# SSD stage: the sample's in-chunk products join the run of chunks 2 and 3, over two PSUM banks

## The chip, the cores and the metric

The kernel runs on one core of one Trainium2 chip. The metric is device time in microseconds (us) of one execution. Below, PE is TensorE, DVE is VectorE, ACT is ScalarE, POOL is GpSimd, and SP is SyncE, whose queue issues most of the DMAs. PEld in the profile is the weight load that belongs to each matmul.

## The reference, cut to what matters

One decoder layer computes `proj = rmsnorm(x) @ w_in` for 512 prompt tokens and for a sample batch of 8 rows of 8 tokens (64 tokens), runs three branches, merges them and projects. The change is in branch B, the Mamba-2 SSD. It has 32 heads in 8 groups of 4, head dimension 64 and state size 128. Per group and per chunk of 128 tokens:

```
a_cs   = cumsum(dt * a)
y_diag = einsum('bclgn,bcsgn->bgcls', c, b) * exp(a_cs[l] - a_cs[s], l >= s) @ (x * dt)
states = einsum('bcsgn,bgrcs,bcsgrp->cbgrpn', b, exp(a_cs[-1] - a_cs), x * dt)
y_off  = c @ h_prev * exp(a_cs);  h = h * exp(a_cs[-1]) + states
y      = y_diag + y_off + x * d_skip
```

The prompt is chunks 0 to 3. The 64 sample tokens are handled as a fifth chunk, number 4, whose mask keeps the 8 rows apart and whose carried state comes from `state_ssm`.

## The kernel before

The stage before the change's stage normalises x and holds its transpose in two parts (`hn_hi`, `hn_lo`); every large product takes three matmul passes (hi by hi, hi by lo, lo by hi). The SSD stage then goes through the 8 groups. PE's order is written out by hand: a list `units` alternates half jobs of the large products (24 matmuls of 128x288 into an `acc` bank, function `gemm_half`, line 167; some 3.2 us) with lists of SSD steps, the function `steps(g)` (line 778) with twelve of them, `w[0]` to `w[11]`, for each group. The half jobs that run beside group g make the convolution inputs of group g+1 (`conv_job`), the gate z of group g (`z_job`) and, from group 2 on, parts of the output projection (`proj_job`). Weights for a job are loaded two jobs ahead by SP (line 130) and split one job ahead into `whi` (ACT, line 98) and `wlo` (DVE, line 99). The order on DVE, ACT and SP is not written out: a scheduler places their instructions from its own estimate, so it may move work far from the edit. Each engine then runs its list strictly in order.

The steps named in this document, with the lines of the kernel before:

- `decays(g, c)`, lines 480 to 492: a DMA brings the decay exponents of chunk c into a tile `e` (three buffers), DVE adds the mask (L489), ACT takes four exponentials (L491).
- `chunk_cb(g, c)`, line 524: PE forms C by B (L532), DVE multiplies `e` by it (L533). The last instruction is kept as `made`.
- `y_diag(g, cs)`, line 536: for each chunk and each of the four heads one matmul with 64 output partitions (L548, `yps<-e,xdt`). In the trace each of these f32 matmuls shows as two. `run(first, ...)` makes the first matmul wait for the `made` of the other chunks, so that PE does not stop inside the run.
- `y_add`, line 554: DVE adds the bank to `ysb` (L559).
- `c_h0(g, j)`, line 664: eight matmuls with 32 output partitions (L674) into a `yps` bank; ACT copies it out (L678).
- `h0_T`, `h0_new`: transposes of the sample's states (L644), their update (PE L653, ACT L658, DVE L659).
- `gate_y(g-1)`, `norm_y(g-1)`: gate and group norm of the group before; ACT takes Ln (L701) and Exp (L702), with a load of the function table wherever one follows another kind.

There are 8 PSUM banks: 3 `acc`, 2 `yps`, 3 `sps`. In a group `yps` is taken five times, in the order chunks 0 and 1, chunks 2 and 3, `c_h0` 0, `c_h0` 1, chunk 4.

Of the kernel before, what the change touches and what calls it, by code (L numbers as in the profile page):

```python
# [17 lines left out]
P = 128  # L18
# [3 lines left out]
TS = 64  # L22
# [20 lines left out]
def tile_hybrid_step(  # L43
# [8 lines left out]
    V, S, PE, GP, SY = nc.vector, nc.scalar, nc.tensor, nc.gpsimd, nc.sync  # L52
# [21 lines left out]
    def y_tile():  # L74
        return bank["yps"].tile([P, 512], F32, tag="yps", name="yps")
# [42 lines left out]
    def run(first, *made):  # L118

        for m in made:  # L120
            tc.add_manual_dep(first.ins, m.ins.name, mybir.DependencyInfo(
                mybir.DependencyClass.NoSync if m.ins.engine == first.ins.engine else mybir.DependencyClass.Sync,
                mybir.DependencyReason.DATA), reason="run")
# [76 lines left out]
    with ExitStack() as stb:  # L200
# [17 lines left out]
        for i in range(5):  # L218
# [6 lines left out]
            r = rsqrt_(pb, ss[:n], 1.0 / D, EPS, "BT", root=True)  # L225
# [120 lines left out]
        for f in range(2):  # L346
            PE.matmul(rps[:96, 128 + f * H:128 + (f + 1) * H], lhsT=sel[:, f].rearrange("p r t -> p (r t)"),
                      rhs=wdec[:, 4], start=True, stop=True)
# [131 lines left out]
        def decays(g, c):  # L480

            d = st_[g]
            h0_ = 4 * g
            smp = c == 4
            w = TS if smp else P
            e = d["ex", c] = pb.tile([P, 4, P], F32, tag="e", name="e", bufs=3)
            ew = e[:, :, 0:w]
            SY.dma_start(out=ew, in_=a_scr[h0_:h0_ + 4, c * P:c * P + w][None].to_broadcast([P, 4, w]))
            V.tensor_tensor(ew, ew, (tri4 if smp else tri)[:, None, 0:w].to_broadcast([P, 4, w]), ALU.add)  # L489
            for h in range(4):  # L490
                S.activation(e[:, h, 0:w], e[:, h, 0:w], AF.Exp, bias=nacs[:, c, h0_ + h:h0_ + h + 1])  # L491
# [41 lines left out]
            made = V.tensor_tensor(ew, ew, cb[:, None, 0:w].to_broadcast([P, 4, w]), ALU.mult)  # L533
            d["e", c] = e, d.pop(("xdt", c)), made

        def y_diag(g, cs):

            d = st_[g]
            yps = y_tile()
            w = TS if cs[0] == 4 else P  # L540
            y4 = yps[:, 0:2 * len(cs) * w].rearrange("p (c j l) -> p c j l", c=len(cs), j=2)
            parts = [d.pop(("e", c)) for c in cs]
            first = None
            for i, (e, xdt, made) in enumerate(parts):
                for j in range(2):
                    for r in range(2):
                        h = 2 * j + r
                        m = PE.matmul(y4[64 * r:64 * r + 64, i, j], lhsT=xdt[:, h], rhs=e[:, h, 0:w], start=True, stop=True)  # L548
                        first = first or m
            if len(parts) > 1:  # L550
                run(first, *[p[2] for p in parts[1:]])
            return y4

        def y_add(g, cs, y4):
            ysb = st_[g]["ysb"]
            w = y4.shape[3]
            c0 = cs[0] * P
            dst = ysb[:, :, c0:c0 + len(cs) * w].rearrange("p j (c l) -> p c j l", c=len(cs))
            V.tensor_tensor(dst, dst, y4, ALU.add)  # L559
# [25 lines left out]
        def y_off(g, c):  # L585

            d = st_[g]
            c0 = c * P
            hT, ysb = d["hT", c - 1], d["ysb"]
            yo = s_tile()  # L590
            for j in range(2):
                PE.matmul(yo[:, j * P:(j + 1) * P], lhsT=hT[:, 2 * j:2 * j + 2].rearrange("p h d -> p (h d)"),  # L592
                          rhs=d["C"][:, c0:c0 + P], start=True, stop=True)
            t1 = pb.tile([P, 2, P], F32, tag="t1", name="t1", bufs=2)
            V.tensor_tensor(t1, yo[:, 0:256].rearrange("p (j l) -> p j l", j=2), d["ebc"][:, :, c0:c0 + P], ALU.mult)
            ys = ysb[:, :, c0:c0 + P]
            V.tensor_tensor(ys, ys, t1, ALU.add)
# [165 lines left out]
        with tc.manual_schedule(engines={mybir.EngineType.PE}):  # L763
            def group_jobs(g):

                c = [conv_job(g + 1, ci) for ci in range(4)] if g + 1 < G else [gate_job(0), gate_job(1), gate_job(2), gate_job(3)]
                z = [z_job(g, 0), z_job(g, 1)]
                if g < 2:
                    return c + z
                p = [proj_job(g // 2 - 1, 2 * (g % 2) + i) for i in range(2)]  # L770
                if g % 2 == 0:
                    return c + [z[0], p[0], z[1], p[1]]
                return [c[0], p[0], c[1], p[1], c[2], c[3]] + z

            def yd(g, *cs):
                y_add(g, cs, y_diag(g, cs))

            def steps(g):

                w = [[] for _ in range(12)]  # L780
                w[0] = [lambda: start_y(g), lambda: decays(g, 2), lambda: chunk_a(g, 1)]
                w[1] = [lambda: state(g, 0)]
                if g > 0:
                    w[1] += [lambda: y_smp(g - 1), lambda: gate_y(g - 1)]
                w[2] = [lambda: state(g, 1), lambda: chunk_a(g, 2)]
                w[3] = [lambda: y_off(g, 1), lambda: yd(g, 0, 1), lambda: decays(g, 3)]
                w[4] = [lambda: state(g, 2), lambda: chunk_a(g, 3), lambda: decays(g, 4)]
                if g > 0:
                    w[5] = [lambda: norm_y(g - 1)]
                w[5] += [lambda: y_off(g, 2), lambda: chunk_a(g, 4), lambda: h0_load(g, 0)]  # L790
                w[6] = [lambda: state(g, 3), lambda: chunk_t4(g), lambda: h0_load(g, 1)]
                w[7] = [lambda: y_off(g, 3), lambda: chunk_cb(g, 4)]
                w[8] = [lambda: yd(g, 2, 3), lambda: state_out(g), lambda: h0_T(g, 0, 0)]
                w[9] = [lambda: h0_T(g, 0, 1), lambda: h0_new(g, 0, 0), lambda: h0_new(g, 0, 1)]
                w[10] = [lambda: c_h0(g, 0), lambda: h0_T(g, 1, 0), lambda: h0_T(g, 1, 1)]
                if g + 1 < G:
                    w[10] += [lambda: decays(g + 1, 0), lambda: decays(g + 1, 1)]
                w[11] = [lambda: h0_new(g, 1, 0), lambda: h0_new(g, 1, 1)]
                if g + 1 < G:
                    w[11] += [lambda: conv_out(g + 1)]  # L800
                w[11] += [lambda: c_h0(g, 1), lambda: yd(g, 4)]
                return w


            units = [(j, h) for j in (conv_job(0, ci) for ci in range(4)) for h in range(2)]
            units.append((None, [lambda: decays(0, 0), lambda: decays(0, 1)]))
            for g in range(G):
                us = [(j, h) for j in group_jobs(g) for h in range(2)]
                w = steps(g)
                at = range(12) if g < 2 else (0, 1, 3, 4, 6, 7, 9, 10, 11, 13, 14, 15) if g % 2 else (0, 1, 2, 3, 4, 5, 7, 9, 10, 12, 13, 15)  # L810
                at = list(at)
                if g == 0:
                    at = [min(a + 1, 11) for a in at]
                    between = {0: [lambda: chunk_a(0, 0), lambda: conv_out(0)]}
                else:
                    between = {}
                    units.append((None, [lambda g=g: chunk_a(g, 0)]))
                for i, a in enumerate(at):
                    between.setdefault(a, []).extend(w[i])
                for u, x in enumerate(us):  # L820
                    units += [x, (None, between.get(u, []))]
            tail = {0: [lambda: y_smp(G - 1), lambda: gate_y(G - 1)], 5: [lambda: norm_y(G - 1)]}
            for i, u in enumerate([(j, h) for j in (gate_job(jj) for jj in range(4, 8)) for h in range(2)]):
                units += [u, (None, tail.get(i, []))]
            units += [(j, h) for j in (proj_job(3, p) for p in range(4)) for h in range(2)]

            jobs = [u[0] for u in units if u[0] is not None and u[1] == 0]
            at = {id(j): i for i, j in enumerate(jobs)}
            jobs[0].load()
            jobs[0].prep()  # L830
            jobs[1].load()
            for j, h in units:
                if j is None:
                    for w_ in h:
                        w_()
                    continue
                i = at[id(j)]
                if h == 0:
                    if i + 2 < len(jobs):
                        jobs[i + 2].load()  # L840
                    if i + 1 < len(jobs):
                        jobs[i + 1].prep()
                j.half(h)
# [509 lines left out]
    for a in range(2):  # L1353
        r, c = slice(64 * a, 64 * a + 64), slice(512 * a, 512 * a + 512)
# [139 lines left out]
```

## Time and profile before

| what | value |
|---|---|
| median of 3 runs | 1150.23 us (1148.32 to 1156.42) |
| the profiled execution, its own time | 1151.22 us |
| its span, first to last instruction | 1149.5 us |
| mean granted TensorE clock | 0.993 of 2.4 GHz |
| PE busy | 1099.6 us, 96% of the span |
| DVE busy | 781.9 us, 68% |
| ACT busy | 622.1 us, 54% |

The span is shorter than the time by 1.7 us that lie around the instructions. A row of the timeline gives start, duration, engine, line, operation, output and inputs, count, and in brackets the idle time before it with what ended that idle time. "issue" there means that nothing in the profile was waited for.

### The profile page before, as it was taken

The numbers are of one execution on the slowest core, as the hardware profiler recorded it, in microseconds if no ns is written. First come the engines' busy times: TensorE is split into PE (matmuls) and PEld (weight loads), VectorE is DVE, ScalarE is ACT, GpSimd is POOL, SyncE is SP. The second block draws the span as 40 slices with busy tenths as digits, with TensorE's granted clock in tenths as the row PEclk, the third lists the DMA queues.
The fourth block names the chain that finished last, engine by engine and source line by source line (L and its number), as shares of the span: only waits on it lengthen the run. The fifth ranks groups of instructions, "written<-read, shape, count | busy, mean of one in ns | idle before, by whom it ended". The sixth has DMA issues, their size and how long they took to land.

```text
span 1149.5 us, 20445 instructions
## 1 busy us (share of the span) xinstructions
PE 1099.6 (96%) x8199; PEld 1024.1 (89%) x8199; DVE 781.9 (68%) x1450; ACT 622.1 (54%) x1294; POOL 37.7 (3%) x110
## 2 busy tenths in 40 slices
PE   5989999899999989989999999999999999999997
PEld 4989899799998989989999877899999999889776
DVE  5778787748787667866644644786875567775743
ACT  6456686766868456665553244344653236564421
POOL 3010010000000000000000000000000000000000
PEclk9999999999999999999999999999999999999999
DMA  6433544155352524425232525631262353465411
GB/s 190 128 82 111 156 116 138 59 159 145 98 156 84 155 88 126 126 70 169 88 115 95 190 74 165 193 111 52 96 222 101 130 180 102 121 183 197 152 47 73
DMA packets 160462, 144.90 MB, mean 126 GB/s; under 512 B 10160, under 2 KB 141264, under 8 KB 160368
## 3 DMA queue, kind: packets, MB, share of 16 engines
q1 hardware_dynamic: 137264, 126.12, 35.9%
q10 hardware_dynamic: 23104, 17.49, 4.8%
q8 instruction: 64, 1.05, 0.4%
q14 instruction: 30, 0.25, 0.1%
HBM read 124.13 MB, written 19.46 MB: 125 GB/s over the span
## 4 chain that ended last, share of the span: by engine, by line
PE 84%; DVE 6%; ACT 5%; DMA 3%; issue 1%; ACTq 0%; SPq 0%
PE acc L167 32%; PE acc L908 15%; PE acc L154 12%; PE acc L1038 4%; PE acc L1443 4%; PE acc L1103 2%; PE yps L548 2%; DVE cacc L418 1%; PE sps L644 1%; DVE wlo L99 1%; PE sps L503 1%; PE sps L567 1%; PE sps L592 1%; PE yps L674 1%; PE yps L1391 1%
## 5 line engine op out<-in xcount | busy, mean ns | idle before, releaser
L167 PE MATMUL acc<-hn_hi,whi 128*128 128x288 f32 x896 | 272.6, 304 | 1.0 <-ACT thm L732 0.8
L167 PE MATMUL acc<-hn_hi,wlo 128*128 128x288 f32 x896 | 266.2, 297 | 4.1 <-DVE wlo L99 4.1
L167 PE MATMUL acc<-hn_lo,whi 128*128 128x288 f32 x896 | 265.7, 297 | 0.0
L167 PEld LDWEIGHTS acc<-hn_hi,wlo 128*128 128x128 f32 x896 | 169.7, 189 | 4.4 <-DVE wlo L99 4.3
L167 PEld LDWEIGHTS acc<-hn_hi,whi 128*128 128x128 f32 x896 | 170.1, 190 | 3.6 <-ACT thm L732 1.0
L167 PEld LDWEIGHTS acc<-hn_lo,whi 128*128 128x128 f32 x896 | 170.0, 190 | 0.5
L98 ACT CAST w<-wraw 128x1024 fp32r<-128x1024 f32 (+1 forms) x64 | 59.2, 942 | 103.4 <-PE acc L908 24.0
L99 DVE TENSOR_TENSOR wlo<-wraw,whi 128x1024 fp32r<-128x1024 f32 x72 | 87.9, 1221 | 31.8 <-ACT whi L98 31.3
L167 PE MATMUL acc<-hb,whi 128*128 128x288 f32 x512 | 105.2, 301 | 3.1 <-DVE zs L463 2.6
L98 ACT CAST whi<-wraw 128x1024 fp32r<-128x1024 f32 x72 | 75.5, 1049 | 56.1 <-PE acc L167 48.3
L99 DVE TENSOR_TENSOR w<-wraw,w 128x1024 fp32r<-128x1024 f32 x64 | 68.5, 1087 | 36.0 <-ACT w L98 35.9
L908 PE MATMUL acc<-hn_hi,w 128*128 128x288 f32 x512 | 89.5, 300 | 0.0
L908 PE MATMUL acc<-tT,w 128*128 128x288 f32 x576 | 86.1, 298 | 0.0
L167 PEld LDWEIGHTS acc<-hb,whi 128*128 128x128 f32 x512 | 82.7, 191 | 3.7 <-DVE zs L463 2.8
L418 DVE SCALAR_TENSOR_TENSOR cacc<-raw,cwh,cacc 128x600 f32<-128x600 f32 x96 | 80.3, 838 | 4.2 <-ACT cacc L416 3.7
L908 PEld LDWEIGHTS acc<-tT,w 128*128 128x128 f32 x576 | 78.5, 188 | 0.9 <-issue 0.9
L167 PE MATMUL acc<-hb,wlo 128*128 128x288 f32 x256 | 76.0, 297 | 2.8 <-DVE wlo L99 2.8
L908 PEld LDWEIGHTS acc<-hn_hi,w 128*128 128x128 f32 x512 | 74.1, 188 | 2.1 <-DVE thx L926 0.5
L491 ACT ACTIVATE e<-e,nacs 128x128 f32<-128x128 f32 (+1 forms) x160 | 50.3, 386 | 16.4 <-DVE e L489 16.4
L99 DVE TENSOR_TENSOR w<-S,w 128x1024 fp32r<-128x1024 f32 x32 | 39.2, 1224 | 25.1 <-ACT w L98 25.1
L167 PEld LDWEIGHTS acc<-hb,wlo 128*128 128x128 f32 x256 | 48.8, 191 | 3.1 <-DVE wlo L99 3.1
L154 PE MATMUL acc<-ha,w 128*128 128x288 f32 x384 | 51.5, 295 | 0.0
(392 smaller groups left out, 2137.6 us busy)
## 6 DMA issues: line engine op xcount, KB each, us to landing
wraw<-in_w_in_dram SPq DMA_DIRECT2D x44, 1024.0 KB
wraw<-in_w_in_dram SPq DMA_DIRECT2D x16, 512.0 KB
e<-a_scr SPq DMA_DIRECT2D x32, 256.0 KB
h<-in_state_ssm_dram SPq DMA_DIRECT2D x16, 512.0 KB
out_dram<-h ACTq DMA_DIRECT2D x16, 512.0 KB
wraw<-in_w_proj_b_dram SPq DMA_DIRECT2D x8, 1024.0 KB
ebc<-e_scr SPq DMA_DIRECT2D x16, 288.0 KB
wraw<-in_w_mem_kv_dram SPq DMA_DIRECT2D x4, 1024.0 KB
```

Of the source, the lines that this page charges most:

```text
L98: S.copy(hi, v)
L99: (e or V).tensor_tensor(lo, v, hi, ALU.subtract)
L154: PE.matmul(ps[:n, :width], lhsT=a, rhs=b[:, sl], start=(i == 0), stop=(i == last))
L167: PE.matmul(ps[:, 0:HT], lhsT=a[:, k], rhs=b(k)[:, sl], start=(n == 0), stop=(n == 3 * nk - 1))
L418: V.scalar_tensor_tensor(a[:, 0:n], raw[:, i:i + n], cwh[:, i, q:q + 1], a[:, 0:n], ALU.mult, ALU.add)
L491: S.activation(e[:, h, 0:w], e[:, h, 0:w], AF.Exp, bias=nacs[:, c, h0_ + h:h0_ + h + 1])
L503: PE.transpose(tp[:, j * P:(j + 1) * P], xs[:, j, c0:c0 + P], ident)
L548: m = PE.matmul(y4[64 * r:64 * r + 64, i, j], lhsT=xdt[:, h], rhs=e[:, h, 0:w], start=True, stop=True)
L908: PE.matmul(ps[:, 0:HT], lhsT=w[:, r, k], rhs=x(q, k), start=first and n == 0, stop=n == 11, skip_group_check=True)
L1038: PE.matmul(pss[i], lhsT=x(k)[:, c], rhs=w[:, r, k2], start=(k + q == 0), stop=(k == KD - 1 and q == 2))
L1103: PE.matmul(pss[i], lhsT=x[xr], rhs=w[:, r, k2], start=(k + q == 0), stop=(k == KD - 1 and q == 2))
L1443: PE.matmul(ps[:, 0:cn], lhsT=x(k)[:, c], rhs=w, start=(k + q == 0), stop=(k == KD - 1 and q == 2))
```

## The change

`y_diag` and `yd` now take several tuples of chunks. Each tuple gets a `yps` bank of its own, all their matmuls follow one another, and the first of them waits for the `made` of every chunk but the first. Step `w[8]` calls it for chunks 2 and 3 and, in a second bank, chunk 4. The call for chunk 4 at the end of `w[11]` is gone. The number of matmuls, additions, banks and DMAs is as before.

```
-        def y_diag(g, cs):
+        def y_diag(g, *parts_):
             d = st_[g]
-            yps = y_tile()
-            ...
-            if len(parts) > 1:
-                run(first, *[p[2] for p in parts[1:]])
-            return y4
+            first, made_, y4s = None, [], []
+            for cs in parts_:
+                yps = y_tile()
+                ...
+                for i, c in enumerate(cs):
+                    e, xdt, made = d.pop(("e", c))
+                    made_.append(made)
+                    ...
+            run(first, *made_[1:])
+            return y4s
...
-            def yd(g, *cs):
-                y_add(g, cs, y_diag(g, cs))
+            def yd(g, *parts_):
+                for cs, y4 in zip(parts_, y_diag(g, *parts_)):
+                    y_add(g, cs, y4)
...
-                w[8] = [lambda: yd(g, 2, 3), lambda: state_out(g), lambda: h0_T(g, 0, 0)]
+                w[8] = [lambda: yd(g, (2, 3), (4,)), lambda: state_out(g), lambda: h0_T(g, 0, 0)]
...
-                w[11] += [lambda: c_h0(g, 1), lambda: yd(g, 4)]
+                w[11] += [lambda: c_h0(g, 1)]
```

PE, end of group 0 (from `w[10]` on), before. The names after the arrow are the tiles read; `x8` counts matmuls of the program.

```order
L674 MATMUL yps<-h0T,C 32x128 x8
L644 MATMUL sps<-ident,h_1230 128x128 x8
L653 MATMUL sps<-btd,xst 128x512 x2
L438 MATMUL sps<-ident,cg 108x128
L674 MATMUL yps<-h0T,C 32x128 x8
L548 MATMUL yps<-e,xdt 64x64 x4
L503 MATMUL sps<-ident,xs 128x128 x3
```

In the changed kernel the four 64x64 matmuls no longer stand between `c_h0` (L674) and the transposes of the next group (L503). PE, the run in `w[8]` of group 0, as it is now (L551 is the old L548, L582 the old L580):

```order
L167 MATMUL acc<-hn_hi,wlo 128x288
L551 MATMUL yps<-e,xdt 64x128 x8
L551 MATMUL yps<-e,xdt 64x64 x4
L582 MATMUL sps<-ident,hT 128x128 x2
L646 MATMUL sps<-ident,h_1169 128x128 x4
```

They stand directly behind the eight 64x128 ones, three steps earlier in the list. The same holds in all eight groups.

SP, from group 0 into group 1: its list before,

```order
L130 DMA wraw<-in_w_in_dram 128x8x128 x2
L488 DMA e<-a_scr 128x4x128 x2
L637 DMA h_1882<-in_state_ssm_dram 128x8x128
L488 DMA e<-a_scr 128x4x128
L637 DMA h_1939<-in_state_ssm_dram 128x8x128
```

and now:

```order
L130 DMA wraw<-in_w_in_dram 128x8x128 x2
L488 DMA e<-a_scr 128x4x128 x3
L639 DMA h_1882<-in_state_ssm_dram 128x8x128
L639 DMA h_1939<-in_state_ssm_dram 128x8x128
```

The load of the next group's chunk 2 into the buffer that chunk 4 frees moves ahead of a load of states, up to the loads for chunks 0 and 1.

ACT, group norm inside group 2 (Ln, exponentials of chunk 4, Exp), before:

```order
L701 ACT_TABLE_LOAD
L701 ACTIVATE zs<-acc 128x288
L416 ACTIVATE cacc<-raw,cbh,cwh 128x600
L511 COPY BT<-sps 128x128
L701 ACTIVATE zs<-acc 128x288
L491 ACT_TABLE_LOAD
L491 ACTIVATE e<-e,nacs 128x64 x4
L702 ACTIVATE zs<-zs 128x576
```

and now (L703 and L704 are the old L701 and L702):

```order
L703 ACT_TABLE_LOAD
L703 ACTIVATE zs<-acc 128x288
L511 COPY BT<-sps 128x128
L491 ACT_TABLE_LOAD
L491 ACTIVATE e<-e,nacs 128x64 x4
L416 ACTIVATE cacc<-raw,cbh,cwh 128x600
L703 ACT_TABLE_LOAD
L703 ACTIVATE zs<-acc 128x288
L626 CAST xst<-xv 96x256
L704 ACT_TABLE_LOAD
L704 ACTIVATE zs<-zs 128x576
```

The exponentials of chunk 4 now stand between the two Ln, with four table loads in place of two. This is a consequence that the scheduler drew, not an edit; groups 4 and 6 had four before and have four now.

## Rows read from the trace of the kernel before

**Rows 1.** The page, part 1: busy us, share of span, instructions.

```profile
span 1149.5 us, 20445 instructions
PE 1099.6 (96%) x8199; PEld 1024.1 (89%) x8199; DVE 781.9 (68%) x1450; ACT 622.1 (54%) x1294; POOL 37.7 (3%) x110
```

**Rows 2.** Weight loads beside chunk 4's products, group 2; L644 behind a c_h0.

```profile
248.55 0.31 PEld L548 LDWEIGHTS yps<-e,xdt 128*64 128x64 f32 x8 [0.20 <-issue]
248.93 0.31 PEld L503 LDWEIGHTS sps<-ident,xs 128*128 128x128 f32 x3
...
116.06 0.86 PEld L644 LDWEIGHTS sps<-ident,h 128*128 128x128 f32 x8 [0.20 <-issue]
```

**Rows 3.** Run of chunks 2, 3 (L548) and chunk 4's multiply (L533): groups 0, 1, 3, 4.

```profile
106.39 0.85 PEld L548 LDWEIGHTS yps<-e,xdt 128*64 128x64 f32 x16 [0.16 <-issue]
106.81 0.41 DVE L533 TENSOR_TENSOR e<-e,sps 128x256 f32<-128x256 f32 x1
107.41 0.20 PEld L580 LDWEIGHTS sps<-ident,hT 128*128 128x128 f32 x2 [0.17 <-DVE e L533]
...
160.07 0.85 PEld L548 LDWEIGHTS yps<-e,xdt 128*64 128x64 f32 x16 [0.17 <-issue]
160.58 0.42 DVE L533 TENSOR_TENSOR e<-e,sps 128x256 f32<-128x256 f32 x1
...
295.81 0.85 PEld L548 LDWEIGHTS yps<-e,xdt 128*64 128x64 f32 x16 [0.16 <-issue]
296.63 0.41 DVE L533 TENSOR_TENSOR e<-e,sps 128x256 f32<-128x256 f32 x1
...
360.54 0.41 DVE L533 TENSOR_TENSOR e<-e,sps 128x256 f32<-128x256 f32 x1
361.37 0.85 PEld L548 LDWEIGHTS yps<-e,xdt 128*64 128x64 f32 x16 [0.16 <-issue]
```

**Rows 4.** PE's waits, whole kernel: us in total, times, longest.

```profile
PE sps L503 <- DVE h L659: 2.2, 2, 1.1
```

**Rows 5.** PE's waits around the group norm, groups 2, 4, 6 (timeline).

```profile
215.56 0.61 PE L167 MATMUL acc<-hn_hi,wlo 128*128 128x288 f32 x1 [4.10 <-DVE wlo L99]
359.59 0.53 PE L167 MATMUL acc<-hb,whi 128*128 128x288 f32 x2 [2.57 <-DVE zs L463]
497.95 0.41 PE L532 MATMUL sps<-C,xs 128*128 128x64 f32 x2 [1.09 <-DVE hT L574]
501.52 0.40 PE L167 MATMUL acc<-hb,wlo 128*128 128x288 f32 x1 [2.84 <-DVE wlo L99]
```

**Rows 6.** Windows: stretch, length, busy PE, PEld, DVE, ACT, POOL; clock; DMA share; GB/s.

```profile
120.20:122.20 2.00, 1.95 (x15) 1.84 (x16) 1.70 (x4) 0.69 (x3) 0.00 (x0) 1.00 1.04 304
215.50:217.50 2.00, 1.95 (x8) 1.95 (x9) 2.00 (x5) 2.00 (x6) 0.00 (x0) 0.50 0.03 8
217.50:219.50 2.00, 2.00 (x12) 2.00 (x11) 1.97 (x4) 0.13 (x1) 0.00 (x0) 0.67 0.00 0
359.50:361.50 2.00, 1.91 (x14) 1.75 (x16) 2.00 (x6) 1.18 (x4) 0.00 (x0) 1.00 0.03 8
501.50:503.50 2.00, 1.98 (x10) 1.99 (x11) 1.99 (x6) 1.58 (x4) 0.00 (x0) 0.66 0.00 0
503.50:505.50 2.00, 2.00 (x10) 2.00 (x9) 2.00 (x4) 0.00 (x0) 0.00 (x0) 0.50 0.00 0
```

**Rows 7.** ACT's table loads for Ln, by line: count, ns min/median/max.

```profile
L701 ACT ACT_TABLE_LOAD  x10: 1283/1283/1283, 149.8 to 614.1; - x10
```

**Rows 8.** The page, part 5: DVE's convolution pass; busy us, mean ns, idle before.

```profile
L418 DVE SCALAR_TENSOR_TENSOR cacc<-raw,cwh,cacc 128x600 f32<-128x600 f32 x96 | 80.3, 838 | 4.2 <-ACT cacc L416 3.7
```

**Rows 9.** Loads of e behind the run of group 2, and DVE (timeline).

```profile
227.86 0.95 SPq L488 DMA_DIRECT2D e<-a_scr  x2
233.30 0.69 DVE L489 TENSOR_TENSOR e<-e,tri 128x512 f32<-128x512 f32 x1 [4.31 <-DMA e<-a_scr]
236.50 0.45 DVE L463 SCALAR_TENSOR_TENSOR zs<-th,acc 128x288 f32<-128x288 f32 x1 [0.77 <-ACT th L462]
```

More of the change, by code (lines that the diff above doesn't have):

```diff
@@ L534, in chunk_cb @@
             d["e", c] = e, d.pop(("xdt", c)), made
-        def y_diag(g, cs):
+        def y_diag(g, *parts_):
             d = st_[g]
-            yps = y_tile()
[L540 to L549, printed above, removed]
-            if len(parts) > 1:
-                run(first, *[p[2] for p in parts[1:]])
-            return y4
+            first, made_, y4s = None, [], []
+            for cs in parts_:
+                yps = y_tile()
+                w = TS if cs[0] == 4 else P
+                y4 = yps[:, 0:2 * len(cs) * w].rearrange("p (c j l) -> p c j l", c=len(cs), j=2)
+                y4s.append(y4)
+                for i, c in enumerate(cs):
+                    e, xdt, made = d.pop(("e", c))
+                    made_.append(made)
+                    for j in range(2):
+                        for r in range(2):
+                            h = 2 * j + r
+                            m = PE.matmul(y4[64 * r:64 * r + 64, i, j], lhsT=xdt[:, h], rhs=e[:, h, 0:w], start=True, stop=True)
+                            first = first or m
+            run(first, *made_[1:])
+            return y4s
         def y_add(g, cs, y4):
@@ L785, in steps @@
                 w[2] = [lambda: state(g, 1), lambda: chunk_a(g, 2)]
-                w[3] = [lambda: y_off(g, 1), lambda: yd(g, 0, 1), lambda: decays(g, 3)]
+                w[3] = [lambda: y_off(g, 1), lambda: yd(g, (0, 1)), lambda: decays(g, 3)]
                 w[4] = [lambda: state(g, 2), lambda: chunk_a(g, 3), lambda: decays(g, 4)]
```

## The prediction

> **What bounds the kernel now.** I read the page's busy times first, then PE's list of waits, then the timeline of each group of the SSD stage (60 to 648 us), then windows of 2 us for the clock. PE is busy for 1099.6 of 1149.5 us [rows 1], so the change can win only what PE spends on its products and on the waits in front of them, and it loses whatever new wait it puts in front of PE. DVE at 781.9 us and ACT at 622.1 us have room as a whole, but not everywhere: around the group norm PE waits for them [rows 5]. I hold the sum against the profiled execution, 1151.22 us, which lies 1.0 above the median of the three runs, 1150.23. A change of less than 1% (11.5 us) is about what cannot be told from none.
>
> **Part 1, a mode of PE left out per group.** The four products of chunk 4 (eight weight loads) stood between products with 32 output partitions and transposes with 128. The reader sees 0.20 us of issue gap in front of them, 0.31 us of loads and, from 248.86 to 248.93, 0.07 behind them [rows 2]. Without them the transposes follow the 32-partition products directly; the nearest such place is L644, with a gap of 0.20 [rows 2]. At the new place they follow products of the same shape: the 0.31 us of loads stay, no gap arises in front, and the gap behind the run, 0.17 in front of L580 [rows 3], becomes the 0.07 that now stands behind the 64-column products. So per group 0.20 + 0.07 + 0.17 = 0.44 becomes 0.20 + 0.07 = 0.27: 0.17 saved, times 8 is 1.4 us. If the gap behind the run stays at 0.17 it is 0.07 times 8 = 0.6; if every gap saved is a full 0.20 it is 1.6. The Trainium skill, page "TensorEngine Tiling (Array Packing)", section Key Properties, says that a change of tiling mode drains TensorE. By that rule each change costs alike, and one fewer per group at 0.20 gives 1.6 in place of 1.4; the rows agree in kind, but not that all changes cost the same.
>
> **Part 2, the run waits for one more multiply.** The first matmul of the run now also waits until DVE has multiplied the decays of chunk 4 (L533, the 128x256 form). In the trace of before that multiply ends, against the start of the run, at 107.22 against 106.39 in group 0, 161.00 against 160.07 in group 1 and 297.04 against 295.81 in group 3 [rows 3]. DVE's list up to that point is unchanged in these three groups, so PE stands still for 0.83 + 0.93 + 1.23 = 3.0 us, which I round up to 3.1 for the semaphores. In group 4 the multiply is done 0.42 before the run (360.95 against 361.37) and in the others earlier by more, so they pay nothing. Bounds: 0 if upstream shifts bring the multiply forward, 4.3 if groups 4 and 5 lose their margin and pay as much as group 3 once. Behind the waiting matmul stand the transposes of the states, and with them ACT's and DVE's update of the sample's states; in groups 0 and 1 PE later waits 1.1 us for that update (L503 for L659) [rows 4], so part 1's gain is swallowed there, but ACT's exponentials for the next group leave that place too, and I count the two as equal. Waits of this length leave the clock alone: behind the 1.1 us wait at 120 the granted clock reads 1.00 [rows 6].
>
> **Part 3, the scheduler's new order around the norm.** In groups 2, 4 and 6 PE waits for DVE and ACT behind the norm. Group 2 costs 4.10, and its clock then falls to 1.2 GHz: 0.50 and 0.67 granted over two windows of 2 us, a loss of 1.00 + 0.66 = 1.7, in all 5.8. Group 4 costs 2.57 with the clock at 1.00, say 2.6. Group 6 costs 1.09 + 2.84, and 0.68 + 1.00 = 1.7 of clock, in all 5.6 [rows 5, 6]. Together 14.0. The Trainium skill, page "TensorE: Matmul & The Clock Gate", Part 1, holds that an engine left idle falls to half rate until it has worked for some time; the trace agrees at 4.10 and 2.84 and shows no loss at 2.57. Without the clock the three groups would come to 10.6 in place of 14.0.
> In the changed lists group 4 has the order that group 6 had, word for word up to the run, so I give it 5.6. Groups 2 and 6 come close to the old order of group 4, with DVE's eviction of z behind one more convolution pass of 0.84 us [rows 8]: 2.6 each at best, 2.6 + 0.8 + 1.7 = 5.1 at worst if the longer wait drops the clock. The two extra table loads of group 2, 1.28 each [rows 7], are already in group 4's 2.6, which had four loads. The three then come to 10.8 to 15.8, a change of -3.2 to +1.8; I take the middle, -0.7.
>
> **Part 4, what I cost at nothing.** DVE's addition of chunk 4 (L559) only moves; the second bank is free, since the products of chunks 0 and 1 were added long before, and `c_h0` comes two steps, and so two half jobs, behind the run. The earlier load of the next group's chunk 2 takes a DMA wait out of DVE at the start of a group, where PE did not wait for it; its cover is the half job of some 3.2 us beside it.
>
> **Sum.** 1151.2 - 1.4 + 3.1 - 0.7 = 1152.2 for an execution like the profiled one; less the 1.0 by which it lies above the median, 1151.2. I predict 1151 us: no change that can be told. By the ends of the terms (-1.6 to -0.6, 0 to 4.3, -3.2 to +1.8) this case runs from 1145.4 to 1155.7.
>
> **Rivals.**
> *The third load blocks DVE (slower).* Three loads of `e` now leave SP together behind the run, and DVE takes the mask of the third before it evicts z or the states. In group 2 DVE already stood 4.31 for the first load, 233.30 against an issue at 227.86, and the eviction of z came at 236.50 with 0.77 of slack [rows 9]. A third load adds a pass of 0.69 and between 0 and 2.7 us of transfer (half of the 5.4 us that passed with two in flight). I take 0.7, nearer to the lower end because the second load's mask, behind a `wlo`, shows no wait of its own. That is 1.4 per group and in seven groups 10 us if all of it reached PE: 1151 + 10 = 1161, and 1156 if half does. It decides once that delay exceeds the 0.77 of slack plus the 3.2 us that a half job of PE gives with three `acc` banks. That cushion speaks against it. Chance 0.13.
> *The multiply arrives in time (faster).* Part 2 is worth nothing because DVE, relieved of the DMA wait at the start of the group, runs earlier; parts 1 and 3 stay: 1150.2 - 1.4 - 0.7 = 1148.1. For it: the wait is only about 1 us in each of three groups. Against it: DVE's list in front of the multiply depends on matmuls just before the run. Chance 0.17.
> *The norm of all three groups eases (faster).* If groups 2, 4 and 6 all cost 2.6, part 3 is 7.8 - 14.0 = -6.2: 1150.2 - 1.4 + 3.1 - 6.2 = 1145.7. Against it: group 4 now has the list that cost 5.6. Chance 0.15.
> The forecast keeps 0.55.
>
> **The range** 1145 to 1157 takes in the forecast's own ends, both faster rivals and the lower half of the slower one; the runs of before themselves spread from 1148 to 1156. Faster by over 1% means below 1138.7, beyond even the third rival: 0.03. Slower by over 1% means above 1161.7, which only the full price of the first rival with part 2 on top reaches: 0.04. Within 1%: 0.93.
>
> **What would show it.** In the changed profile: PE idle in front of the run of groups 0, 1 and 3, released by DVE's `e` multiply, 0.8 to 1.3 us each and none in groups 5 and 7; no issue gap between `c_h0` and a 64-column product, and 0.07 in place of 0.17 behind the run; PE's waits in group 4 like those of group 6 before, with a clock below 1.00, and group 2 below 4.1. The prediction would be wrong if PE waited for z evictions behind the run (first rival), if group 2's wait grew, or if the run of groups 4 or 6 began to wait too.

## The result: 0.8% slower, and the profile after

The changed kernel took 1158.92 us (median of 9 runs, 1155.21 to 1167.10) against 1150.76 for the kernel before, run beside it: a ratio of 1.008, with a 95% interval of 1.006 to 1.0099. Run again later it took 1160.00 against 1152.54: 1.0056, 1.0036 to 1.0076. (The ratio is an estimate of its own, not the quotient of the two medians.) The forecast, 1151 in a range of 1145 to 1157, was wrong by about 8 us. The profiled execution of after took 1163.97 us, 5 above its median: at 85 us, before the change does anything, it was already 4.3 us behind. So the reading below is of the SSD stage alone, from 80 us on, and a second profile of after is read beside it.

The page of after: span, busy times with their share, and PE's granted clock in 40 slices; it answers to [rows 1].

```profile
span 1162.3 us, 20464 instructions
PE 1108.3 (95%) x8199; PEld 1032.9 (89%) x8199; DVE 782.1 (67%) x1450; ACT 626.3 (54%) x1296; POOL 39.1 (3%) x110
...
PEclk9989999989998999999999999999999999999999
```

PE has as many matmuls as before and 8.7 us more of busy time. The same work takes longer when the clock is lower (in group 2 of after a matmul of 128x288 shows 0.29 us before the clock fell and 0.44 after it), and three digits of the last row read 8; the first of them, 58 to 87 us, lies ahead of the change.

PE's matmuls that open the run of chunks 2, 3 and 4, where they waited (timeline: start, us, engine, line, operation; in brackets the idle time before it and what ended it); they answer to [rows 3].

```profile
111.58 1.33 PE L551 MATMUL yps<-e,xdt 128*64 128x128 f32 x24 [0.81 <-DVE e L533]
...
167.74 1.32 PE L551 MATMUL yps<-e,xdt 128*64 128x128 f32 x24 [0.91 <-DVE e L533]
...
309.11 1.33 PE L551 MATMUL yps<-e,xdt 128*64 128x128 f32 x24 [1.21 <-DVE e L533]
...
450.86 1.32 PE L551 MATMUL yps<-e,xdt 128*64 128x128 f32 x24 [0.87 <-DVE e L533]
```

Groups 0, 1 and 3 wait as forecast; group 5 does too, which was not: 3.80 us in all.

PE's waits around the group norm and behind the groups' ends, same view; they answer to [rows 5] and [rows 4].

```profile
125.20 0.55 PE L503 MATMUL sps<-ident,xs 128*128 128x128 f32 x3 [0.99 <-DVE h L661]
...
185.50 0.55 PE L503 MATMUL sps<-ident,xs 128*128 128x128 f32 x3 [2.43 <-DVE h L661]
...
229.17 0.41 PE L532 MATMUL sps<-C,xs 128*128 128x64 f32 x2 [0.55 <-DVE hT L576]
230.96 0.40 PE L167 MATMUL acc<-hb,wlo 128*128 128x288 f32 x1 [0.86 <-DVE wlo L99]
234.21 0.85 PE L167 MATMUL acc<-hb,whi 128*128 128x288 f32 x2 [1.04 <-DVE zs L463]
...
369.57 0.41 PE L532 MATMUL sps<-C,xs 128*128 128x64 f32 x2 [1.07 <-DVE hT L576]
373.13 0.61 PE L167 MATMUL acc<-hb,wlo 128*128 128x288 f32 x1 [2.83 <-DVE wlo L99]
...
510.65 0.41 PE L532 MATMUL sps<-C,xs 128*128 128x64 f32 x2 [0.54 <-DVE cg L412]
511.82 0.53 PE L167 MATMUL acc<-hb,whi 128*128 128x288 f32 x2 [0.76 <-ACT whi L98]
514.37 0.40 PE L167 MATMUL acc<-hb,wlo 128*128 128x288 f32 x1 [2.02 <-DVE wlo L99]
```

By waits alone groups 2, 4 and 6 cost 2.45 + 3.90 + 3.32 = 9.7 us, less than the 10.6 before. The price there is in the clock. The same places as windows of 10 us (length; busy us of PE, weight loads, DVE, ACT, POOL with counts; then the granted clock, DMA share, GB/s), which answer to [rows 6]:

```profile
122.00:132.00 10.00, 8.95 (x64) 7.71 (x63) 3.31 (x8) 5.90 (x18) 0.00 (x0) 0.83 0.63 178
184.00:194.00 10.00, 8.45 (x52) 8.22 (x53) 5.32 (x10) 5.27 (x17) 0.00 (x0) 0.83 0.58 164
230.00:240.00 10.00, 8.10 (x54) 7.32 (x54) 8.87 (x18) 6.94 (x18) 2.30 (x5) 0.66 0.01 3
370.00:380.00 10.00, 7.17 (x49) 6.69 (x49) 7.71 (x16) 4.32 (x11) 0.25 (x2) 0.66 0.01 2
430.00:440.00 10.00, 8.06 (x62) 7.83 (x61) 8.51 (x18) 6.79 (x10) 0.48 (x3) 1.00 0.29 93
510.00:520.00 10.00, 6.68 (x45) 6.05 (x46) 9.43 (x20) 6.89 (x15) 0.33 (x1) 0.83 0.00 0
```

A window at 0.83 lost 1.7 us to the lower level of 1.2 GHz, one at 0.66 lost 3.4. In 2 us steps, the third wait of group 2 (1.04, up to 234.21) and half of group 4's second (2.83, up to 373.13) lie where the clock is down already:

```profile
233.00:235.00 2.00, 0.96 (x4) 0.79 (x4) 1.97 (x4) 2.00 (x6) 0.00 (x0) 0.50 0.00 0
...
371.00:373.00 2.00, 0.00 (x0) 0.00 (x0) 1.94 (x4) 1.62 (x5) 0.00 (x0) 0.65 0.00 0
```

One stall of the kernel before stands in no row shown so far. It is in group 5, at the sums of the norm (L699, now L701): the timeline of PE, and a window of 10 us:

```profile
419.51 0.41 PE L699 MATMUL acc<-qq,onesn 128*128 128x288 f32 x1 [3.67 <-DVE m_sb L755]
...
417.00:427.00 10.00, 7.49 (x46) 7.49 (x47) 8.60 (x18) 8.21 (x12) 0.48 (x3) 0.83 0.33 106
```

Waits and clock by place, from such rows of the three profiles (waits + clock, us):

| place | before | after | after, second profile |
|---|---|---|---|
| opening of the run, groups 0, 1, 3, 5 | 0 | 3.8 + 0 | 3.8 + 0 |
| ends of groups 0 and 1 (L503) | 2.2 + 0 | 3.4 + 3.4 | 3.4 + 3.4 |
| norm, group 2 | 4.1 + 1.7 | 2.5 + 3.4 | 2.4 + 3.4 |
| norm, group 4 | 2.6 + 0 | 3.9 + 3.4 | 3.9 + 3.4 |
| group 5 (L699, after L701) | 3.7 + 1.7 | 1.9 + 0 | 2.4 + 0 |
| norm, group 6 | 3.9 + 1.7 | 3.3 + 1.7 | 3.3 + 1.7 |
| sum | 21.6 | 30.8 | 31.1 |

So 9.2 to 9.5 us more, less the mode saved, 1.4: about 8. That is the measured difference: from just before group 0's run to the first product behind the stage, the two profiles of after lose 8.3 and 8.4 us on the one of before. The table is not exact in its parts. Half of the time that PE waits at the lower clock is counted in both columns, some 1.3 us in after and 0.9 in its second profile, and waits under half a microsecond or at other places (0.81 and 0.46 at the start of group 3) are left out. By the table the clock makes up 6.8 of the difference; by the means over many runs, in the next section, 3.5.

### The profile page after: what moved, and what is told of

Same layout as the page of the kernel before. It is cut to its first block, busy times and chain, and to the rows that moved or that the text cites. A ratio compares the mean times of both kernels' runs of the same rounds, so it can differ in the third digit from the quotient of the medians.

```text
span 1162.3 us, 20464 instructions
## 1 busy us (share of the span) xinstructions
PE 1108.3 (95%) x8199; PEld 1032.9 (89%) x8199; DVE 782.1 (67%) x1450; ACT 626.3 (54%) x1296; POOL 39.1 (3%) x110
## 4 chain that ended last, share of the span: by engine, by line
PE 80%; ACT 8%; DVE 8%; DMA 3%; issue 1%; SPq 0%; ACTq 0%; DVEq 0%
PE acc L167 29%; PE acc L911 15%; PE acc L154 12%; PE acc L1041 4%; PE acc L1446 4%; DVE cacc L418 2%; PE acc L1106 2%; PE yps L551 2%; DMA e<-a_scr 2%; DVE wlo L99 1%; PE sps L646 1%; ACT L703 1%; ACT whi L98 1%; PE sps L503 1%; PE sps L569 1%
## 5 line engine op out<-in xcount | busy, mean ns | idle before, releaser
L167 PE MATMUL acc<-hb,whi 128*128 128x288 f32 x512 | 109.0, 308 | 2.3 <-DVE zs L463 1.0
L167 PEld LDWEIGHTS acc<-hb,whi 128*128 128x128 f32 x512 | 85.8, 197 | 3.1 <-DVE zs L463 1.4
```

The costliest lines, as they stand in the source:

```text
L167: PE.matmul(ps[:, 0:HT], lhsT=a[:, k], rhs=b(k)[:, sl], start=(n == 0), stop=(n == 3 * nk - 1))
```

## The experiments

Theories. **W**: the run's wait, with the clock that falls behind it. **C**: the clock falls because chunk 4's products no longer stand between the states and the next group's transposes. **O**: the other engines' new order, with the third load of `e`; it was later narrowed to **N**: their order around the norm. Each execution's span is split in two with its mean granted clock: span × clock is work and waits put to full rate, span × (1 − clock) is what the clock took. Means over all runs of a kernel, less those of the kernel before, run beside it (its own: 1140.3 to 1141.1 and 9.6 to 10.0). The spread of the runs leaves a standard error of about 0.5 us on a difference at full rate and of about 1 us on one of the clock (1.6 and 1.8 for the four runs with idle products). The nine runs of the result itself had 1143.3 and 15.3.

| kernel | runs | median us | ratio to before (95%) | full rate | clock |
|---|---|---|---|---|---|
| after, second time | 12 | 1160.00 | 1.0056 (1.0036 to 1.0076) | +3.8 | +3.5 |
| run waits for chunk 3 alone | 12 | 1154.62 | 1.0019 (1.0003 to 1.0035) | -1.4 | +3.7 |
| before, with the wait alone | 12 | 1155.64 | 1.0023 (1.0003 to 1.0043) | +3.4 | -0.1 |
| after, third load held | 12 | 1156.55 | 1.0037 (1.0020 to 1.0053) | +0.6 | +3.4 |
| after, idle products | 4 | 1169.20 | 1.0133 (1.0102 to 1.0163) | +10.4 | +5.3 |
| load held, chunk 3 alone | 12 | 1153.87 | 1.0012 (0.9994 to 1.0029) | -0.5 | +2.4 |
| multiply one step earlier | 6 | 1160.77 | 1.0067 (1.0042 to 1.0093) | +3.3 | +5.6 |
| the same, load held | 7 | 1159.44 | 1.0064 (1.0038 to 1.0090) | +3.2 | +4.7 |
| before, exponentials behind the norm | 12 | 1145.53 | 0.9945 (0.9927 to 0.9964) | -3.7 | -1.9 |
| after, the same order | 12 | 1145.85 | 0.9948 (0.9928 to 0.9969) | -2.5 | -3.1 |
| the same, chunk 3 alone | 8 | 1145.24 | 0.9936 (0.9914 to 0.9957) | -4.5 | -2.0 |
| the same, load held too | 12 | 1147.94 | 0.9971 (0.9951 to 0.9992) | -3.0 | -0.4 |

**The run waits for chunk 3 alone** (on after):

```
-            run(first, *made_[1:])
+            run(first, *made_[1:len(parts_[0])])
```

> The changed kernel with one wait less: the first matmul of the run waits for chunk 3's multiply alone, and chunk 4's products, behind 16 others, wait for their own. Place of the products and the order of the other engines stay. By the traces the changed kernel lost 8.2 us of the median: 3.4 more of waits and 6.8 more of clock in the SSD stage, less 1.4. Theory W (the run's wait, 0.81 + 0.91 + 1.21 + 0.87 = 3.8 us, and the clock that falls behind it): 1152 to 1155. Theory C (the clock falls because chunk 4's products no longer stand between the states and the next group's transposes): 1155 to 1158, only the waits come back. Theory O (the other engines' new order, with the third load of e): 1155 to 1158 too, with DVE's 2.06 us stand in group 1 still there.

The time is the one that W expected, just under that of C and O. Full rate fell by 5.2 us against after: 3.8 for the run's waits, and 1.2 because the wait behind group 1 fell from 2.43 to 1.22. It is now 1.4 below before, which agrees with the mode saved. But 3.7 us of clock stay. Group 4 in the timeline and as a window of this kernel:

```profile
362.19 0.61 PE L167 MATMUL acc<-hb,wlo 128*128 128x288 f32 x1 [2.84 <-DVE wlo L99]
```

```profile
358.00:368.00 10.00, 6.53 (x34) 6.17 (x35) 8.35 (x17) 5.36 (x14) 0.25 (x2) 0.66 0.01 2
```

The norm of group 4 has the wait and the clock of after although no run waits. So W explains the part at full rate and not the clock.

**The wait alone, on the kernel before**:

```
-                run(first, *[p[2] for p in parts[1:]])
+                run(first, *[p[2] for p in parts[1:]], *([d["e", 4][2]] if cs[0] == 2 else []))
```

> The kernel before with the wait alone: the first matmul of the run of chunks 2 and 3 also waits for chunk 4's multiply, the products of chunk 4 stay where they were. W: the whole price of the wait, 1150.7 + 3 to 6 = 1154 to 1157. C: 3 us of waits and no clock, since the products stand at their old place: about 1153 to 1154. O: the loads of e come as before, so the waits alone, at most 1153.

PE's list of waits (in total, times, longest), and windows at the three waits:

```profile
PE yps L548 <- DVE e L533: 2.9, 3, 1.2
```

```profile
110.00:114.00 4.00, 3.19 (x34) 2.79 (x33) 4.00 (x9) 3.38 (x8) 0.25 (x2) 1.00 0.97 264
165.00:169.00 4.00, 3.09 (x33) 2.90 (x33) 3.91 (x9) 3.71 (x10) 0.00 (x0) 1.00 0.31 49
302.00:306.00 4.00, 3.02 (x32) 2.85 (x33) 3.97 (x11) 3.78 (x8) 0.48 (x3) 1.00 0.28 49
```

Three waits, 2.9 us, clock 1.00 at each, and no more clock lost in the mean of the runs (-0.1, with a standard error of 1.3): the wait costs about its own length, and nothing here shows the clock falling behind it, as W has it. One thing did move with the wait: the norm of group 2 now has three waits (0.55, 0.87 and 1.67) as in after, where before and the kernel without the run's wait have a single one of 4.1.

**The third load held** until the group's last products with the old states (on after; `ld` is decays' load, `"ch"` the last matmul of `c_h0`):

```
+            ld = SY.dma_start(...); c == 2 and g > 0 and run(ld, st_[g - 1]["ch", 1])
...
+            d["ch", j] = m; run(first, d["h0T", j, 1][1])
```

> The changed kernel, but the third load of e (chunk 2 of the next group) is held until PE has done the products with the old states, the last of the group, as the buffer held it before. DVE's and ACT's order is then within some 100 rows of the kernel before, instead of 470 and 550. O: back to 1151 + 3 (the run's waits) - 1.4 = 1152 to 1154. W: 1155 to 1158, the run's waits and the clock behind them stay. C: 1156 to 1159, and the clock still falls at the ends of groups 0 and 1.

3.2 us of full rate came back, the clock's loss not. The wait behind group 1 fell from 2.43 to 0.95: rival 1's mechanism, which the next section shows. The run of group 5 no longer waits, and the norms of groups 2 and 4 wait 0.9 us less. O in the form "the loads" explains a part.

**Idle products at chunk 4's old place** (on after):

```
+        def idle(g):
+            yps = y_tile()
+            for i in range(8):
+                r = i % 2
+                PE.matmul(yps[64 * r:64 * r + 64, 64 * (i // 2):64 * (i // 2) + 64], lhsT=ident[:, 0:64], rhs=tri4, start=True, stop=True)
...
-                w[11] += [lambda: c_h0(g, 1)]
+                w[11] += [lambda: c_h0(g, 1), lambda: idle(g)]
```

> The changed kernel with eight products of 64 columns put back at chunk 4's old place, on constants (the identity and a mask), into a bank that nobody reads: they add some 0.3 us of work and a mode of PE per group, where nothing waits for data. C: the clock at the ends of groups 0 and 1 stays at 1.00, and the time falls to 1153 to 1156 in spite of the added work. W and O: the clock there falls as before, 1159 to 1161.

Its timeline of PE at the end of group 0:

```profile
124.14 0.69 PE L560 MATMUL yps<-tri,ident 128*64 128x64 f32 x16
125.21 0.55 PE L503 MATMUL sps<-ident,xs 128*128 128x128 f32 x3 [0.38 <-DVE h L667]
```

There they shorten the wait from 0.99 to 0.38 and the clock stays, but it falls behind group 1 as in after, the kernel lost 8 to 9 us more, and the clock's loss did not shrink. This speaks against C as the cause of the whole, but it is no clean test: the products also take a `yps` bank, and PE has two waits for ACT's copy `BT` that after does not have (1.45 and 1.80 us). The last experiment tests C better.

**The same kernel again, and both edits together.** The two edits of the first and the third experiment in one kernel leave the moved products and DVE's earlier addition.

> The changed kernel as it is, for its mean clock and a second profile beside the others. So far the span times the mean clock (work and waits, put to full rate) was 1143.3 us and the clock's loss 15.3 in the mean of its 9 runs; the kernel before has 1141.1 and 9.9 in 29 runs. All theories: 1158 to 1162 us with the same two parts. What tells them apart in the profile is the place of the falls: C (chunk 4's products missing at the group's end) has them at the ends of groups 0 and 1 again, N (the other engines' order around the norm) in groups 2 and 4.

> Both edits together: the third load of e held until the group's last product, and the run waits for chunk 3's multiply alone. What is left of the change is the place of chunk 4's products on PE and DVE's earlier addition; DVE and ACT differ from the kernel before in fewer than 80 rows. Work and waits: 1141.1 - 1.4 = 1139.7, as in the kernel that took the wait alone away. Clock: C expects the 3.5 us more of loss that the three kernels with the moved products showed, so 1155 in all; N expects most of it gone, 1151 to 1152.

The second profile of after has its falls at the places of the first (the table above). Both edits together came to 1153.87, 1.0012, an interval that holds no change: between C's 1155 and N's 1151 to 1152, and undecided by itself.

**The multiply one step earlier**, alone and with the load held:

```
-                w[6] = [lambda: state(g, 3), lambda: chunk_t4(g), lambda: h0_load(g, 1)]
-                w[7] = [lambda: y_off(g, 3), lambda: chunk_cb(g, 4)]
+                w[6] = [lambda: state(g, 3), lambda: chunk_t4(g), lambda: chunk_cb(g, 4), lambda: h0_load(g, 1)]
+                w[7] = [lambda: y_off(g, 3)]
```

> The changed kernel with chunk 4's C-B product and its multiply one step earlier (with the states of chunk 3), so that the run finds it done. The run's waits of 0.81 to 1.21 us in groups 0, 1, 3 and 5 go: work and waits near 1139.7. Clock: C 13 to 14 us of loss and so 1154 to 1155; N depends on the order around the norm, which changes again, 1151 to 1156. If the wait moves to another place (the states of chunk 3, or the off-diagonal products), 1157 to 1159.

> The same with the third load of e held as well: no wait at the run, the loads in the old order, chunk 4's products in the run. A version that could beat the kernel before: by work and waits 1139.7 and, by N, the old clock loss of 9.9: 1151.4. By C 1155.

The wait went elsewhere, as the last case of the first expectation had it, and cost more than the 1157 to 1159 given there; with the load held it took 1159.44, 4 us above the upper end of what was expected. PE's timeline in group 4:

```profile
359.60 0.66 PE L532 MATMUL sps<-C,xs 128*128 128x64 f32 x2 [5.74 <-DVE bst L630]
```

PE now reaches chunk 4's C-B product (L532) while DVE still reads the transposes of chunk 4 (`bst`), and stands 5.74 us. One step earlier was too early; it says nothing on C or N.

**Exponentials behind the norm.** In group 4 of after ACT does the norm's first logarithm, chunk 4's four exponentials, the second logarithm, and then the norm's exponential. The timeline of ACT, and DVE's next step in its own:

```profile
354.79 1.28 ACT L703 ACT_TABLE_LOAD   x1
356.08 0.41 ACT L703 ACTIVATE zs<-acc 128x288 f32<-128x288 f32 x1
356.51 1.28 ACT L491 ACT_TABLE_LOAD   x1
357.81 1.07 ACT L491 ACTIVATE e<-e,nacs 128x64 f32<-128x64 f32 x4
358.89 1.28 ACT L703 ACT_TABLE_LOAD   x1
360.19 0.41 ACT L703 ACTIVATE zs<-acc 128x288 f32<-128x288 f32 x1
```

```profile
362.92 1.55 DVE L707 SCALAR_TENSOR_TENSOR ysb<-ysb,gh,zs 128x576 f32<-128x576 f32 x2 [3.63 <-ACT zs L704]
```

DVE stands 3.63 us, and 1.28 + 1.07 + 1.28 = 3.63 us of ACT lie between the logarithms (that the two are equal is chance). (The Trainium skill, page "ScalarE activation tables: per-element evaluation and per-set limits", section What a function is on this engine, puts two functions of different sets one table load of 1283 ns apart; the trace agrees at 1.28.) The edit, on four kernels, orders chunk 4's exponentials of the even groups behind the norm's exponential. In the program's order the whole step `decays(g, 4)`, with its load and its mask, moves one list later:

```
+                ex = S.activation(...); smp and g > 0 and g % 2 == 0 and run(ex, st_[g - 1]["ne"])
...
-            S.activation(rs, rs, AF.Exp, scale=-0.5)
+            d["ne"] = S.activation(rs, rs, AF.Exp, scale=-0.5)
...
+                w[4] = [lambda: state(g, 2), lambda: chunk_a(g, 3)] + [lambda: decays(g, 4)] * (g == 0 or g % 2)
...
+                    w[5] = [lambda: norm_y(g - 1)] + [lambda: decays(g, 4)] * (g % 2 == 0)
```

By the traces it is a narrow edit: on the changed kernel PE's order stays as it is, and some 24 of DVE's 1450 instructions and 42 of ACT's 1404 (DMA issues included) change places, all from group 2 on.

> The kernel before with one order on ACT set by hand: in groups 2, 4 and 6 chunk 4's exponentials come behind the norm's own exponential, in place of between its two logarithms, which saves two table loads of 1.28 us each in front of the norm's result (in group 4 of the traces ACT goes logarithm, load, exponentials, load, logarithm, load, exponential). Products, PE's order and loads are as before. N (the norm's stalls and their clock come from ACT's order there): the waits of 4.10 + 2.57 + 3.93 us shrink to 2 to 4 in all and two falls of the clock (3.4) go: 1152.4 less 7 to 12, 1140 to 1146. If DVE's list and not ACT's is what ends the waits: 1150 to 1153.

> The changed kernel with the same order on ACT. N: the difference between change and no change then lies in the run's waits (3.8), the wait at the end of group 1 (1.3) and the mode saved (-1.4) alone, with no more clock than the kernel before has with this order: 3 to 4 us over that kernel, 1144 to 1150. C (the clock's extra loss belongs to the products' new place): still 7 us over it.

> The changed kernel with the same order on ACT, and the run waits for chunk 3's multiply alone. N: the mode saved is all that is left, 1 to 2 us under the kernel before with this order, 1139 to 1145. C: 2 to 3 us over it.

> The same, and the third load of e is held until the group's last product. N: as without the hold, within 1 us, 1139 to 1145, with DVE closest to its old order. If the third load costs something by itself, it is 1 to 2 us faster than the kernel without the hold. C: 2 to 3 us over the kernel before with this order.

With this order the kernel before takes 1145.53, at the upper end of what N expected (its group 2 still waits 3.51 and loses 3.4 of clock), and the changed one 1145.85: of the 8 us of the change 0.3 are left. Its run still waits, by PE's list of waits:

```profile
PE yps L551 <- DVE e L533: 4.0, 4, 1.4
```

Group 4 of the changed kernel with this order, in the timelines of ACT, of DVE and of PE:

```profile
343.35 1.28 ACT L703 ACT_TABLE_LOAD   x1
344.65 0.71 ACT L703 ACTIVATE zs<-acc 128x288 f32<-128x288 f32 x2
345.38 1.28 ACT L704 ACT_TABLE_LOAD   x1
```

```profile
347.39 1.55 DVE L707 SCALAR_TENSOR_TENSOR ysb<-ysb,gh,zs 128x576 f32<-128x576 f32 x2 [1.01 <-ACT zs L704]
```

```profile
359.09 0.40 PE L167 MATMUL acc<-hb,wlo 128*128 128x288 f32 x1 [1.34 <-DVE wlo L99]
```

DVE's wait falls from 3.63 to 1.01, and PE's two, 1.07 and 2.83, become one of 1.34. The norm of group 2 with this order, in PE's timeline of the kernel before and of the changed one:

```profile
218.93 0.61 PE L167 MATMUL acc<-hn_hi,wlo 128*128 128x288 f32 x1 [3.51 <-DVE wlo L99]
...
217.10 0.40 PE L167 MATMUL acc<-hn_hi,wlo 128*128 128x288 f32 x1 [1.60 <-DVE wlo L99]
```

The changed kernel's windows at the ends of groups 0 and 1 and at the norm of groups 2 and 4:

```profile
120.00:130.00 10.00, 8.96 (x77) 8.22 (x77) 5.21 (x9) 5.65 (x19) 0.00 (x0) 1.00 0.59 171
178.00:188.00 10.00, 7.80 (x69) 7.29 (x61) 4.91 (x10) 5.02 (x17) 0.00 (x0) 1.00 0.46 127
214.00:224.00 10.00, 8.39 (x64) 8.05 (x63) 9.79 (x19) 8.05 (x20) 0.96 (x3) 1.00 0.01 2
356.00:366.00 10.00, 8.66 (x81) 8.20 (x80) 8.13 (x17) 6.01 (x16) 0.25 (x2) 1.00 0.12 24
```

No clock is lost at any of them in this execution, a good one (1143.63 where the median is 1145.85). In the mean of 12 runs the clock took 6.5 us, where the kernel before loses 9.6 and the kernel before with this order 7.7.

Taken together, the price had two parts. The 3.8 us at full rate are the run's waits and the longer wait behind group 1, less the mode: without the run's wait they become -1.4. The 3.5 us of clock are not the run's: they stay without its wait (+3.7) and do not come with the wait alone (-0.1). Nor are they the products' new place as such: with the other order on ACT the changed kernel loses 1.2 us less clock than the kernel before (standard error 1.0). N holds for them: they come with the norm's chain. It is not the amount of reordering either: the change moves some 234 instructions on DVE and 275 on ACT, and with the other order on ACT, where it costs 0.3 us, 235 and 272.

N's size for the changed kernel was 3 to 4 us too high in the difference (0.3 measured; full rate +1.2, clock -1.2). The run's waits are still paid, but the norms of groups 2, 4 and 6 wait 2.9 us in the changed kernel and 5.3 in the kernel before, both with the new order. So the change is not free there; it is paid out of stalls that are shorter. With the wait taken out as well the kernel reaches 1145.24, ratio 0.9936 to the kernel before (expected 1139 to 1145, and 1 to 2 us under the kernel before with this order), and all three versions beat both kernels; among themselves they cannot be told apart. Holding the load on top brought nothing: 1147.94, against the expected 1139 to 1145.

## Why the prediction was wrong, step by step

**Part 1 (-1.4) had the mechanism, and its size is not contradicted.** Behind the run of after, in the timeline of the weight loads, which answers to [rows 2, 3]:

```profile
112.29 0.48 PEld L551 LDWEIGHTS yps<-e,xdt 128*64 128x64 f32 x10
112.83 0.20 PEld L582 LDWEIGHTS sps<-ident,hT 128*128 128x128 f32 x2
```

The gap is 0.06 where it was 0.17. Without the wait, full rate lies 1.4 below the kernel it is compared with (0.5 with the load held, 0.8 with the exponentials behind the norm), each with a standard error of 0.3 to 0.6. These differences also hold the other waits that moved, so no run measures the mode alone.

**Part 2 (+3.1) had the mechanism and nearly the size**: 3.80 in the trace, since group 5 lost its margin, inside the bound of 4.3; +3.4 at full rate when done alone. That waits of this length leave the clock alone held for the run's waits. At the place from which it was read, the wait behind group 0, it did not: there the clock fell behind 0.99 us in both profiles of after.

**Part 3 (-0.7) is the step that failed.** It gave groups 2, 4 and 6 a cost of 10.8 to 15.8 after the change; they cost 5.9 + 7.3 + 5.0 = 18.2, against 14.0 before. The waits were forecast well: 9.7 us, group by group close to the list. The clock was not: the forecast had falls of 1.7 us, one where a wait is long and none where it is short, from [rows 6], in all 1.7 to 5.1 for the three norms, and 3.4 + 3.4 + 1.7 = 8.5 were lost. In group 4 waits of 1.07 and 2.83 lost 3.4, in all three profiles that have them there, where group 6 before had lost 1.7 behind nearly the same two. In group 2 the clock had fallen after waits of 0.55 and 0.86 already, and 3.4 were lost where the single wait of 4.10 lost 1.7. (The Trainium skill, page "TensorE: Matmul & The Clock Gate", Part 1, "A second HAM failure mode: psum-queue depth-cycling", tells of a kernel whose PE idles shortly but often and swings between the two rates. In group 2 of after the clock fell once; that this is the page's case is not shown.) Group 5, which the sum did not price, gained 3.0 to 3.5; that was luck, and it hides part of the miss.

By the means of many runs the change cost 3.8 us at full rate and 3.5 of clock, where the sum had 1.0 in all.

**Part 4 (nothing) was wrong at one place.** Rival 1's mechanism, chance 0.13, is there in group 1 of after, in DVE's timeline:

```profile
178.40 0.69 DVE L489 TENSOR_TENSOR e<-e,tri 128x512 f32<-128x512 f32 x1 [2.06 <-DMA e<-a_scr]
179.01 0.68 DVE L661 TENSOR_TENSOR h<-h,sps 128x512 f32<-128x512 f32 x1
```

The mask of the third load stands 2.06 us for its transfer, the states' update queues behind it, and PE's wait grew from 1.08 to 2.43 with 1.7 of clock. It is one group and not seven; it came through the states, not the evictions of z.

**The range** ended at 1157, short by 2: its upper case had the run's wait and falls of 1.7 in groups 2, 4 and 6, but no fall of 3.4 and none at the ends of groups 0 and 1. The other two rivals did not come: the multiply was late in four groups, and the norm got dearer.

**What stays open.** Why 3.4 and not 1.7 us of clock are lost behind a given set of waits was not settled, and one profile does not give the price of a wait. PE's waits at the norm of groups 2 and 4 and the clock lost there (windows of 10 us), in all profiles but the two with the multiply one step earlier:

| profile | group 2: waits | clock | group 4: waits | clock |
|---|---|---|---|---|
| before | 4.10 | 1.7 | 2.57 | 0 |
| before, with the wait alone | 0.55, 0.87, 1.67 | 1.7 | 2.50 | 0 |
| after | 0.55, 0.86, 1.04 | 3.4 | 1.07, 2.83 | 3.4 |
| after, second profile | 0.55, 0.87, 0.96 | 3.4 | 1.08, 2.84 | 3.4 |
| run waits for chunk 3 alone | 4.11 | 1.7 | 1.08, 2.84 | 3.4 |
| third load held | 0.55, 0.87, 0.72 | 3.4 | 0.54, 0.77, 2.01 | 1.7 |
| load held, chunk 3 alone | 3.90 | 3.4 | 0.53, 0.77, 2.02 | 1.7 |
| idle products | 0.55, 0.87, 1.66 | 1.7 | 0.47, 0.77, 2.02 | 1.7 |
| before, exponentials behind the norm | 3.51 | 3.4 | 0.40 | 0 |
| after, the same order | 1.60 | 0 | 1.34 | 0 |
| the same, chunk 3 alone | 4.09 | 3.4 | 1.34 | 0 |
| the same, load held too | 3.96 | 3.4 | 1.72 | 0 |

In group 2 a single wait of about 4 us lost 1.7 in two profiles and 3.4 in three, and three short waits 1.7 in two and 3.4 in three. Group 4 is steadier: its clock goes with its waits. It is the place where the change made the norm dearer each time.

At the ends of groups 0 and 1 the two profiles of after lost 1.7 each behind waits of 0.99 and 2.4; the changed kernel with the other order on ACT, the same program up to there, waited 0.99 and 2.16 and lost nothing. So part of the table's 6.8 us is chance of the execution; the means of the runs give 3.5 us of clock to the change, with a standard error of about 1. A remainder of C is not excluded either: at these two places the clock fell in six of the eleven profiles with the products at their new place and in none of the three with the old, too few to tell it from chance; and of the versions with the other order on ACT the one with the load held too lost 1.5 us more clock than the kernel before with that order, with a standard error of 0.7.

## What to carry to other kernels

A change on the bound engine also reorders the others where a scheduler places them, and that can cost more than the change: here 1.4 us saved and 3.8 us of new waits ended as some 8 us, in part because a chain that was already late (norm, ACT's tables, weight split) got later. Find the stall that is paid already and ease it first: ACT's order at the norm was worth 6 us by itself, and with it the change's price fell to 0.3. Price waits with the clock that may fall behind them, and in the mean of many runs, not from one profile.

## What the runs showed that was not expected

- In all fourteen profiles of this case the SSD stage's loss to the clock came as a whole number of times 1.71 us, to 0.03: 3 before, 7 and 7 in after, 0 in the changed kernel with the exponentials behind the norm.
- Three short waits at the norm of group 2 (0.55, 0.87 and 0.7 to 1.7 us) cost as much clock as one of 3.9 to 4.1: 1.7 us in two profiles of five and 3.4 in three, for either. Cutting a wait in pieces did not save the clock.
- Work put in to keep PE busy (eight products of 64 columns per group) cost 8 to 9 us net on top of after, with the bank and the waits that came with it, and bought back no clock.
